# Where the weight buffers and working slots of a two-model forward pass lie in the on-chip memory

## The chip, the cores and the metric

The kernel runs on one core of one Trainium2 chip. The metric is the device time of one execution in microseconds (us). A core has a matrix engine (PE, TensorE), a vector engine (DVE), a scalar engine (ACT), a general engine (POOL) and a queue engine that issues transfers (SP). All of them read operands from the on-chip memory of 128 partitions; an address below is a byte offset within a partition, and the *phase* of a buffer is its address modulo 512.

## The reference

Two models of two layers each run one behind the other on 512 tokens of width 1024, everything in float32. What takes the time is matrix products of the activations with some 300 MB of weights.

```
for l in range(DEPTH):                                   # first model
    h = rmsnorm(x, g_mix); z = h @ w_in
    ya = sliding_window_sink_attention(aq, ak, av, sinks) @ w_a
    yb = (retention(rq, rk, rv) * silu(rg)) @ w_b
    x = x + (sigmoid(ga) * ya + sigmoid(gb) * yb) @ w_out
    x = x + square(relu(rmsnorm(x, g_mlp) @ w_up)) @ w_down
x = rmsnorm(x, g_final)
for l in range(DEPTH):                                   # second model
    y = hybrid_mixer(x, ...)     # top-k attention and gated linear attention
    x = layer_norm(ALPHA * x + y)
    y = conv_ffn(x, ...)         # width 2816, a causal convolution of 3 taps, gelu
    x = layer_norm(ALPHA * x + y)
```

## The kernel before

**Products in three parts.** A float32 product is made of three matmuls of type float32r. Each operand is split into a rounded high part and a low remainder: for activations `xh`, `xl` (`split`, L456 to L466), for weights `hi`, `lo`. A step of a product adds w_hi·xh, w_hi·xl and w_lo·xh into one PSUM bank.

**Two forms of product.** In `fm` the weights are stationary: a step (`k_step`, L395 to L397) loads 128x128 weights and streams 512 tokens of `xh` or `xl` past them (in places only 256 tokens). One output tile of a product over 1024 inputs is 8 steps, that is 24 matmuls, and uses exactly one piece of weights. In `tm` the activations are stationary and 256 columns of weights stream (L448 to L450); one output tile there, too, is 24 matmuls, and uses two pieces, the first for steps 0 to 3 and the second for steps 4 to 7. In the profile's rows a matmul's form is written out<-moving,stationary: `pm<-xh,hi` is a step of `fm`, `pm<-hi,xh` one of `tm`.

**Where weights lie.** A piece of weights is 128x1024 floats. A transfer on SP's queue brings two pieces into one of two `raw` buffers. `split_next` then makes `hi` (ACT, L331) and `lo` (DVE or POOL, L332). The *plain* pieces go round four pairs of buffers of 4096 bytes: the i-th plain piece lies in pair i mod 4, counted from 0. When all four pairs are taken, a piece goes into four working slots instead (`whi`, `wlo`, L341 and L342). A working slot is 2048 bytes; there are 75, and everything else lives in them, above all each `xh` and `xl`.

**Addresses.** The eight weight buffers are pools of their own, with padding between them, so that they start at eight different phases from the start of the first: `WT_PHASE = (0, 32, 64, 128, 256, 384, 448, 480)`, the first four for `hi` of pairs 0 to 3, the last four for `lo`. The built program puts the first at 40352, which is phase 416, and the slots at 73632, also phase 416. Since slots are 2048 bytes long, every slot has phase 416. Relative to any slot, pair 0 lies at 0 (`hi`) and 256 (`lo`), pair 1 at 32 and 384, pair 2 at 64 and 448, pair 3 at 128 and 480. A step within a piece moves the stationary operand by 512 bytes, so its phase stays that of its buffer.

**Order.** The order on every engine is the order in which the program is written (`manual_schedule`). Each stage writes the matmuls of its products with the work of the other parts (attention, retention, norms) pumped between output tiles; nothing in that order depends on addresses. Buffers are handed out in rotation as they come free.

Of the kernel before, what the change touches and what calls it, by code (L numbers as in the profile page):

```python
# [12 lines left out]
F = mybir.dt.float32  # L13
FR = mybir.dt.float32r
# [5 lines left out]
P = 128  # L20
# [6 lines left out]
HI_BUFS = 4  # L27
RAW_BUFS = 2
AHEAD_1, AHEAD_2 = 9, 11
WT_PHASE = (0, 32, 64, 128, 256, 384, 448, 480)  # L30
TOP_ROUNDS = 2
NSLOT = 75
FT = 22
GROUPS = ((0, 6), (6, 14), (14, 22))
ALPHA = (2.0 * DEPTH) ** 0.25
# [111 lines left out]
class Small:  # L147


    def __init__(self):  # L150
        self.parts, self.at, self.n = [], {}, 0
# [103 lines left out]
class Net:  # L255
    def __init__(self, nc, tc, pools, meta, w):
        self.nc, self.tc, self.meta, self.w = nc, tc, meta, w
        self.pools = pools
        self.uid = 0
        self.pump = Pump()  # L260
        self.lo_pool = False
        cols = meta["pieces"]
        self.piece_cols = cols
        self.chunk_off, off = [], 0
        self.chunk_cols = []
        for i in range(0, len(cols), 2):
            n = sum(cols[i : i + 2])
            self.chunk_off.append(off)
            self.chunk_cols.append(n)
            off += n * P  # L270
        self.n_dma = self.n_split = self.n_use = 0
        self.raw, self.ready = {}, {}
        self.n_plain = 0
        self.plain = set()
        self.ahead = HI_BUFS
        self.post, self.due, self.later = deque(), [], []
# [35 lines left out]
    def split_next(self, done, pool=False):  # L312


        i = self.n_split
        if i >= len(self.piece_cols):
            return
        c, j = i // 2, i % 2
        while self.n_dma <= min(c + RAW_BUFS - 1, len(self.chunk_off) - 1):
            self.dma_next()  # L320
        o = self.piece_cols[i - 1] if j else 0
        n = self.piece_cols[i]
        raw = self.raw[c][:, o : o + n]
        e = self.nc.gpsimd if pool or self.lo_pool else self.nc.vector
        self.plain = {q for q in self.plain if q >= done}
        if len(self.plain) < HI_BUFS:
            j = self.n_plain % HI_BUFS
            self.n_plain += 1
            hi = self.pools["wt"][j].tile([P, 1024], FR, tag="hi", name=self.name("hi"))
            lo = self.pools["wt"][HI_BUFS + j].tile([P, 1024], FR, tag="lo", name=self.name("lo"))  # L330
            self.nc.scalar.copy(hi[:, :n], raw)  # L331
            e.tensor_tensor(lo[:, :n], raw, hi[:, :n].bitcast(F), op=ALU.subtract)  # L332
            his = [hi[:, :512], hi[:, 512:]]
            los = [lo[:, :512], lo[:, 512:]]
            self.plain.add(i)
        else:
            his, los = [self.s(FR, "whi") for _ in range(2)], [self.s(FR, "wlo") for _ in range(2)]
            for q in range(2):
                r = raw[:, 512 * q : min(512 * q + 512, n)]
                m = r.shape[1]  # L340
                self.nc.scalar.copy(his[q][:, :m], r)  # L341
                e.tensor_tensor(los[q][:, :m], r, his[q][:, :m].bitcast(F), op=ALU.subtract)  # L342
        self.ready[i] = (his, los)
        self.n_split += 1
# [1242 lines left out]
def emit(nc, meta, arrays, stop=None):  # L1587
    ins = {}
    for n, a in arrays.items():
        ins[n] = nc.dram_tensor(n, a.shape, mybir.dt.from_np(a.dtype), kind="ExternalInput").ap()  # L1590
    out = nc.dram_tensor("out", (P, NK, T), F, kind="ExternalOutput").ap()
    with tile.TileContext(nc) as tc:
        with (
            tc.tile_pool(name="raw", bufs=RAW_BUFS) as raw,
            tc.tile_pool(name="const", bufs=1) as const,
            tc.tile_pool(name="tiny", bufs=40) as tiny,
            tc.tile_pool(name="main", bufs=2, space=PSUM) as main,
            tc.tile_pool(name="side", bufs=6, space=PSUM) as side,
            ExitStack() as stack,
        ):  # L1600
            smalls = const.tile([P, arrays["small"].shape[1]], F, name="smalls")
            wt = []
            at = 0

            def pad(n):
                if n:
                    stack.enter_context(tc.tile_pool(name=f"pad{len(wt)}_{n}", bufs=1)).tile([P, n // 4], F, name=f"pad{len(wt)}_{n}")

            for i, ph in enumerate(WT_PHASE):
                pad((ph - at) % 512)  # L1610
                at = ph
                wt.append(stack.enter_context(tc.tile_pool(name=f"wt{i}", bufs=1)))
            pad(-at % 512)
            with tc.tile_pool(name="s", bufs=NSLOT) as sp, tc.manual_schedule():
                pools = dict(raw=raw, wt=wt, const=const, tiny=tiny, main=main, side=side, s=sp)
                net = Net(nc, tc, pools, meta, ins["w"])
                x = [net.s(base="x") for _ in range(NK)]
                net.smalls = smalls
                g0 = const.tile([P, NK], F, name="g0")
                o, n = meta["small"]["g_mix0"]  # L1620
                nc.sync.dma_start(g0, ins["small"][:, o : o + n])
                nc.sync.dma_start(x[0], ins["x"][:, 0, :])
                net.dma_next(True)
                for k in range(1, 4):
                    nc.sync.dma_start(x[k], ins["x"][:, k, :])
                net.dma_next()
                for k in range(4, NK):
                    nc.sync.dma_start(x[k], ins["x"][:, k, :])
                nc.sync.dma_start(smalls, ins["small"])
                net.pos = ins["pos"]  # L1630
                net.ident, net.ones = net.small("ident"), net.small("ones")
                net.tables_1(ins["big"], ins["band"])
                net.ones_r, net.suffix = [const.tile([P, P], FR, name=n) for n in ("ones_r", "suffix_r")]
                net.halves = const.tile([P, 32], FR, name="halves_r")
                nx = {"xs": [None] * 8}
                nx["xs"][0] = net.split(x[0], g0[:, 0:1])
                for _ in range(2):
                    net.split_next(0)
                for k in range(1, NK):
                    nx["xs"][k] = net.split(x[k], g0[:, k : k + 1])  # L1640
                    if k < 7:
                        nx["acc"] = net.sumsq(x[k - 1], nx.get("acc"))
                net.split_next(0)
                for k in range(6, NK):
                    nx["acc"] = net.sumsq(x[k], nx["acc"], nc.vector)
                net.split_next(0)
                nc.scalar.copy(net.ones_r, net.ones)
                nc.scalar.copy(net.suffix, net.small("suffix"))
                nc.scalar.copy(net.halves, net.small("halves"))
                for l in range(DEPTH):  # L1650
                    nx = net.layer_1(l, x, nx)
                xs, iq = nx
                for l in range(DEPTH):
                    xs, iq = net.layer_2(l, xs, iq, ins["wg"], out if l + 1 == DEPTH else None)
# [10 lines left out]
```

## Time and profile before

| | |
|---|---|
| time, median of 3 runs | 3425.09 us (3424.93 to 3425.33) |
| profiled execution | 3424.1 us |
| its span, first to last instruction | 3422.3 us |
| PE busy | 3377.3 us (99%) |
| DVE, ACT, POOL busy | 1969.8, 1293.5, 656.6 us |
| mean granted PE clock | 0.996 |
| transferred | 295.93 MB, 86 GB/s on average |

Matmuls overlap: a row's duration of one matmul includes what it shares with its neighbours, and its end is modelled. The time that a matmul costs is the distance from its start to the start of the next. A stretch that runs from the first matmul of an output tile to the first matmul of the next is therefore the time of one tile, and the rows below are cut that way.

### The profile page before, as it was taken

The numbers are of one execution on the slowest core, as the hardware profiler recorded it, in microseconds if no ns is written. First come the engines' busy times: TensorE is split into PE (matmuls) and PEld (weight loads), VectorE is DVE, ScalarE is ACT, GpSimd is POOL, SyncE is SP. The second block draws the span as 40 slices with busy tenths as digits, with TensorE's granted clock in tenths as the row PEclk, the third lists the DMA queues.
The fourth block names the chain that finished last, engine by engine and source line by source line (L and its number), as shares of the span: only waits on it lengthen the run. The fifth ranks groups of instructions, "written<-read, shape, count | busy, mean of one in ns | idle before, by whom it ended". The sixth has DMA issues, their size and how long they took to land.

```text
span 3422.3 us, 43082 instructions
## 1 busy us (share of the span) xinstructions
PE 3377.3 (99%) x17450; PEld 2813.5 (82%) x17450; DVE 1969.8 (58%) x3435; ACT 1293.5 (38%) x2206; POOL 656.6 (19%) x447
## 2 busy tenths in 40 slices
PE   9999999999999999999999999999999999999997
PEld 7888888887888888889988778888889777888887
DVE  7555543456555553356885447555778844575466
ACT  3433333233333333233533343343354333443342
POOL 5100000123100010030551014210146400232113
PEclk9999999999999999999999999999999999999999
DMA  4222222232122222231222131223212112312230
GB/s 149 75 74 86 87 99 99 93 127 76 50 74 74 99 101 88 98 125 62 75 74 74 62 123 50 87 99 123 99 52 75 64 73 74 124 46 90 99 135 25
DMA packets 44935, 295.93 MB, mean 86 GB/s; under 512 B 5120, under 2 KB 7296, under 8 KB 10816
## 3 DMA queue, kind: packets, MB, share of 16 engines
q1 hardware_dynamic: 44496, 292.66, 23.6%
q8 instruction: 137, 2.24, 0.3%
q14 instruction: 62, 0.51, 0.0%
q10 hardware_dynamic: 160, 0.26, 0.0%
q0 software_dynamic: 80, 0.26, 0.0%
HBM read 291.06 MB, written 2.10 MB: 86 GB/s over the span
## 4 chain that ended last, share of the span: by engine, by line
PE 93%; DVE 5%; issue 1%; ACT 1%; POOL 0%; DMA 0%; DVEq 0%; SPq 0%; ACTq 0%; POOLq 0%
PE pm L395 23%; PE pm L397 22%; PE pm L396 22%; PE ps L397 3%; PE ps L395 3%; PE ps L396 3%; PE pm L448 3%; PE pm L450 2%; PE pm L449 2%; PE ps L544 2%; PE ps L403 1%; PE ps L1091 1%; DVE s L1011 1%; PE ps L404 1%; PE ps L405 1%
## 5 line engine op out<-in xcount | busy, mean ns | idle before, releaser
L395 PE MATMUL pm<-xh,hi 128*128 128x512 f32 (+1 forms) x3056 | 1201.5, 393 | 3.7 <-DVE c L1410 3.1
L397 PE MATMUL pm<-xh,lo 128*128 128x512 f32 (+1 forms) x3056 | 1193.6, 391 | 0.4 <-DVE lo L332 0.4
L396 PE MATMUL pm<-xl,hi 128*128 128x512 f32 (+1 forms) x3056 | 1189.6, 389 | 1.6 <-DVE xl L1563 1.2
L395 PEld LDWEIGHTS pm<-xh,hi 128*128 128x128 f32 x3056 | 574.7, 188 | 134.7 <-issue 12.0
L396 PEld LDWEIGHTS pm<-xl,hi 128*128 128x128 f32 x3056 | 573.9, 188 | 128.3 <-DVE xl L1563 3.2
L397 PEld LDWEIGHTS pm<-xh,lo 128*128 128x128 f32 x3056 | 573.5, 188 | 128.2 <-DVE lo L332 0.8
L332 DVE TENSOR_TENSOR lo<-raw,hi 128x1024 fp32r<-128x1024 f32 (+1 forms) x413 | 515.7, 1251 | 174.8 <-ACT hi L331 173.7
L331 ACT CAST hi<-raw 128x1024 fp32r<-128x1024 f32 (+1 forms) x469 | 483.3, 1036 | 211.0 <-PE pm L396 168.8
L448 PE MATMUL pm<-hi,xh 128*128 128x256 f32 x768 | 219.3, 286 | 1.0 <-DVE s L1009 0.6
L450 PE MATMUL pm<-hi,xl 128*128 128x256 f32 x768 | 216.1, 281 | 0.0
L449 PE MATMUL pm<-lo,xh 128*128 128x256 f32 x768 | 215.1, 280 | 0.0
L395 PE MATMUL pm<-xh,whi 128*128 128x512 f32 (+1 forms) x512 | 186.8, 365 | 4.0 <-DVE s L537 4.0
L396 PE MATMUL pm<-xl,whi 128*128 128x512 f32 (+1 forms) x512 | 186.2, 364 | 0.8 <-DVE xl L1563 0.5
L397 PE MATMUL pm<-xh,wlo 128*128 128x512 f32 (+1 forms) x512 | 185.5, 362 | 0.0
L1418 POOL TENSOR_TENSOR c<-c,c 128x512 f32<-128x512 f32 x44 | 84.4, 1919 | 509.1 <-DVE c L1410 486.3
L332 POOL TENSOR_TENSOR lo<-raw,hi 128x1024 fp32r<-128x1024 f32 x56 | 140.0, 2504 | 128.1 <-ACT hi L331 87.1
L448 PEld LDWEIGHTS pm<-hi,xh 128*128 128x128 f32 x768 | 144.9, 189 | 8.2 <-issue 2.6
L395 PE MATMUL ps<-xh,hi 128*128 128x512 f32 (+1 forms) x384 | 139.0, 362 | 7.4 <-ACT hi L331 7.4
L449 PEld LDWEIGHTS pm<-lo,xh 128*128 128x128 f32 x768 | 145.4, 189 | 0.2
L450 PEld LDWEIGHTS pm<-hi,xl 128*128 128x128 f32 x768 | 144.6, 188 | 0.0
L501 POOL TENSOR_TENSOR s<-s,s 128x512 f32<-128x512 f32 x26 | 35.1, 1351 | 569.6 <-ACT s L498 569.3
L1409 DVE SCALAR_TENSOR_TENSOR c<-pm,smalls,c 128x511 f32<-128x511 f32 x82 | 61.4, 749 | 140.7 <-ACT c L1408 140.6
(318 smaller groups left out, 4784.6 us busy)
## 6 DMA issues: line engine op xcount, KB each, us to landing
raw<-w SPq DMA_DIRECT2D x265, 1024.0 KB, 4.8
raw<-w SPq DMA_DIRECT2D x7, 768.0 KB, 4.4
x<-x SPq DMA_DIRECT2D x8, 256.0 KB, 6.8
out<-acc SPq DMA_DIRECT2D x16, 128.0 KB, 1.8
raw<-w SPq DMA_DIRECT2D x2, 896.0 KB, 4.5
s<-big SPq DMA_DIRECT2D x6, 256.0 KB, 5.9
raw<-w SPq DMA_DIRECT2D x2, 512.0 KB, 5.3
smalls<-small SPq DMA_DIRECT2D x1, 462.5 KB, 7.7
```

The costliest lines, as they stand in the source:

```text
L331: self.nc.scalar.copy(hi[:, :n], raw)
L332: e.tensor_tensor(lo[:, :n], raw, hi[:, :n].bitcast(F), op=ALU.subtract)
L395: mm(ps[:, ts], lhsT=w1, rhs=xh[:, ts], start=first, stop=False)
L396: mm(ps[:, ts], lhsT=w1, rhs=xl[:, ts], start=False, stop=False)
L397: mm(ps[:, ts], lhsT=w2, rhs=xh[:, ts], start=False, stop=last)
L448: self.nc.tensor.matmul(ps[:, :256], lhsT=x1, rhs=w1, start=(k == 0), stop=False)
L449: self.nc.tensor.matmul(ps[:, :256], lhsT=x1, rhs=w2, start=False, stop=False)
L450: self.nc.tensor.matmul(ps[:, :256], lhsT=x2, rhs=w1, start=False, stop=(k == NK - 1))
L501: (e or self.nc.gpsimd).tensor_tensor(acc, acc, sq, op=ALU.add)
L544: self.nc.tensor.transpose(dst[:, i * P : (i + 1) * P], src, self.ident)
L1409: nc.vector.scalar_tensor_tensor(c[:, 1:], ps[:, : T - 1], w[1], c[:, 1:], op0=ALU.mult, op1=ALU.add)
L1418: nc.gpsimd.tensor_tensor(a, a, c, op=ALU.mult)
```

## The change

The eight pools and the padding between them go. One padding of 96 bytes takes their place, then one pool of four `hi` buffers and one of four `lo` buffers. The built program now puts the `hi` buffers at 40448 and on, the `lo` buffers at 56832 and on, and the slots at 73216 and on, all at phase 0. Relative to any slot every weight buffer lies at 0. The raw buffers, the constants and the small tables stay where they were (`raw` and `smalls` at phase 128). What was saved on padding makes room for a 76th slot.

Every engine has the same instructions in the same order with the same shapes, and the i-th plain piece still goes to the buffer i mod 4. Since 76 slots go round in place of 75, a new tile takes another slot than before, and some writes on DVE, ACT and POOL wait for another engine's release; no wait of a PE or SP instruction changes.

```diff
-WT_PHASE = (0, 32, 64, 128, 256, 384, 448, 480)
+PAD = 24
 TOP_ROUNDS = 2
-NSLOT = 75
+NSLOT = 76
...
         if len(self.plain) < HI_BUFS:
-            j = self.n_plain % HI_BUFS
-            self.n_plain += 1
-            hi = self.pools["wt"][j].tile([P, 1024], FR, tag="hi", name=self.name("hi"))
-            lo = self.pools["wt"][HI_BUFS + j].tile([P, 1024], FR, tag="lo", name=self.name("lo"))
+            hi = self.pools["hi"].tile([P, 1024], FR, tag="hi", name=self.name("hi"))
+            lo = self.pools["lo"].tile([P, 1024], FR, tag="lo", name=self.name("lo"))
...
-            for i, ph in enumerate(WT_PHASE):
-                pad((ph - at) % 512)
-                at = ph
-                wt.append(stack.enter_context(tc.tile_pool(name=f"wt{i}", bufs=1)))
-            pad(-at % 512)
+            stack.enter_context(tc.tile_pool(name="pad", bufs=1)).tile([P, PAD], F, name="pad")
+            hi = stack.enter_context(tc.tile_pool(name="hi", bufs=HI_BUFS))
+            lo = stack.enter_context(tc.tile_pool(name="lo", bufs=HI_BUFS))
```

## Rows read from the trace of the kernel before

**Rows 1.** The page: busy time by engine, and the chain that ended last.

```profile
PE 3377.3 (99%) x17450; PEld 2813.5 (82%) x17450; DVE 1969.8 (58%) x3435; ACT 1293.5 (38%) x2206; POOL 656.6 (19%) x447
...
PE 93%; DVE 5%; issue 1%; ACT 1%; POOL 0%; DMA 0%; DVEq 0%; SPq 0%; ACTq 0%; POOLq 0%
```

**Rows 2.** Stretches: from:to, length, busy us (instructions) by engine, clock, DMA share, GB/s.

```profile
817.00:830.00 13.00, 9.04 (x37) 7.08 (x36) 13.00 (x16) 4.71 (x7) 11.41 (x9) 0.95 0.22 82
830.00:1744.00 914.00, 913.82 (x4834) 771.19 (x4834) 504.31 (x920) 327.26 (x577) 143.32 (x100) 1.00 0.24 85
1744.00:1784.00 40.00, 35.90 (x212) 29.27 (x213) 37.26 (x58) 15.83 (x28) 25.14 (x13) 0.96 0.21 76
...
2654.00:2706.00 52.00, 47.51 (x306) 39.54 (x305) 47.91 (x90) 19.75 (x36) 27.51 (x14) 0.97 0.23 82
```

**Rows 3.** Waits of PE, first two: line and what for, us, times, longest us.

```profile
PE ps L1198 <- DVE S L1188: 7.6, 2, 3.8
PE ps L395 <- ACT hi L331: 7.4, 1, 7.4
```

**Rows 4.** PE in four tiles of `fm`: pieces 47 to 50, pairs 3, 0, 1, 2.

```profile
334.22:339.78 5.57, 5.57 (x25) 1.00 0.14 18
339.78:345.23 5.45, 5.45 (x25) 1.00 0.42 174
345.23:350.80 5.57, 5.57 (x25) 1.00 0.09 25
350.80:356.36 5.56, 5.56 (x25) 1.00 0.40 168
```

**Rows 5.** PE in a tile of `fm` with its weights in slots.

```profile
729.17:734.62 5.45, 5.45 (x25) 1.00 0.45 177
```

**Rows 6.** Timeline of the same stretch, its first matmul: start us, us.

```profile
729.17 0.39 PE L395 MATMUL pm<-xh,whi 128*128 128x512 f32 x1
```

**Rows 7.** Groups by line and form: instructions, busy us, mean ns of one.

```profile
L395 PE MATMUL pm<-xh,hi 128*128 128x512 f32 x2968 | 1176.2, 396 | 3.7 <-DVE c L1410 3.1 <-DVE s L537 0.6
...
L448 PE MATMUL pm<-hi,xh 128*128 128x256 f32 x768 | 219.3, 286 | 1.0 <-DVE s L1009 0.6 <-ACT V L1305 0.4
...
L395 PE MATMUL pm<-xh,whi 128*128 128x512 f32 x376 | 147.9, 393 | 4.0 <-DVE s L537 4.0
...
L395 PE MATMUL ps<-xh,hi 128*128 128x512 f32 x264 | 105.3, 399 | 7.4 <-ACT hi L331 7.4
...
L395 PE MATMUL ps<-xh,whi 128*128 128x512 f32 x88 | 34.3, 389 | 0.0
...
L395 PE MATMUL ps<-xh,hi 128*128 128x256 f32 x120 | 33.7, 281 | 0.0
...
L395 PE MATMUL pm<-xh,hi 128*128 128x256 f32 x88 | 25.4, 288 | 0.0
```

**Rows 8.** Timeline, a tile of `tm` on pairs 0 and 1: start us, us.

```profile
131.60 0.28 PE L448 MATMUL pm<-hi,xh 128*128 128x256 f32 x1
...
133.04 0.28 PE L448 MATMUL pm<-hi,xh 128*128 128x256 f32 x1
...
134.47 0.38 PE L544 MATMUL ps<-smalls,s 128*128 128x128 f32 x2
```

**Rows 9.** Timeline, a tile of `tm` on pairs 2 and 3.

```profile
108.66 0.28 PE L448 MATMUL pm<-hi,xh 128*128 128x256 f32 x1
...
111.47 0.38 PE L544 MATMUL ps<-smalls,s 128*128 128x128 f32 x2
```

**Rows 10.** Timeline of DVE: `lo` of pieces 48 and 51, pairs 0 and 3.

```profile
333.02 1.23 DVE L332 TENSOR_TENSOR lo<-raw,hi 128x1024 fp32r<-128x1024 f32 x1 [0.25 <-ACT hi L331]
...
347.76 1.23 DVE L332 TENSOR_TENSOR lo<-raw,hi 128x1024 fp32r<-128x1024 f32 x1 [1.64 <-ACT hi L331]
```

**Rows 11.** Timeline of PE: float32 matmuls on slots, two to a row.

```profile
199.08 0.59 PE L661 MATMUL ps<-rv,s 128*128 128x256 f32 x2
199.51 0.59 PE L665 MATMUL ps<-rv,s 128*128 128x256 f32 x2
```

More of the change, by code (lines that the diff above doesn't have):

```diff
@@ L272, in __init__ @@
         self.raw, self.ready = {}, {}
-        self.n_plain = 0
         self.plain = set()
@@ L1601, in emit @@
             smalls = const.tile([P, arrays["small"].shape[1]], F, name="smalls")
[L1602 to L1607, printed above, removed]
-            for i, ph in enumerate(WT_PHASE):
-                pad((ph - at) % 512)
-                at = ph
-                wt.append(stack.enter_context(tc.tile_pool(name=f"wt{i}", bufs=1)))
-            pad(-at % 512)
+            stack.enter_context(tc.tile_pool(name="pad", bufs=1)).tile([P, PAD], F, name="pad")
+            hi = stack.enter_context(tc.tile_pool(name="hi", bufs=HI_BUFS))
+            lo = stack.enter_context(tc.tile_pool(name="lo", bufs=HI_BUFS))
             with tc.tile_pool(name="s", bufs=NSLOT) as sp, tc.manual_schedule():
-                pools = dict(raw=raw, wt=wt, const=const, tiny=tiny, main=main, side=side, s=sp)
+                pools = dict(raw=raw, hi=hi, lo=lo, const=const, tiny=tiny, main=main, side=side, s=sp)
                 net = Net(nc, tc, pools, meta, ins["w"])
```

## The prediction, made before the changed kernel ran

> **What bounds the kernel now.** I read the busy times and the chain first: PE is busy in 99% of the span, and the chain that ended last is PE for 93% [rows 1]. The cut by stretches says where this doesn't hold [rows 2]: in a long one (914 us) PE is idle for 0.2 us and DVE busy for 504, while at 817, 1744 and 2654 us DVE is busy for nearly all of the stretch and PE misses about 4 us in each. All of PE's idle time is 3422.3 - 3377.3 = 45 us [rows 1], and its two costliest waits come to 7.6 us and to 7.4, the latter once, at the start [rows 3]. The granted clock is 1.00 in the long stretch, that is 2.4 GHz, so nothing is to be had there. What is left is the distance from one matmul to the next. The change alters no matmul, so the question is whether that distance depends on where operands lie.
>
> It does, and the kernel before shows it, since its four pairs of buffers lie at four different phases relative to the slots. In four output tiles in a row, each 24 equal matmuls without an interruption, pair 0 takes 5.45 us and pairs 3, 1 and 2 take 5.57, 5.57 and 5.56 [rows 4]. DMA traffic doesn't explain it: it is heavy (168 to 174 GB/s) in the tile of pair 0 and in that of pair 2. Where the weights lie in slots (0 relative to the streamed slot, as all weights will after the change) a tile takes 5.45 as well [rows 5]; that it is a slot tile is seen in the form of its matmuls [rows 6]. So relative phases 0 and 256 cost 5.45 / 24 = 227 ns a matmul, the others 232 ns. In the long undisturbed stretches the 5 ns repeat with each round of four tiles.
>
> **Edit 1: the weight buffers go to relative phase 0; stationary weights, 512 tokens.** This form on plain buffers has 2968 + 264 = 3232 steps of three matmuls [rows 7], or 404 tiles of 8 steps; the other two lines of a step have the same counts. A quarter of them is on pair 0 and stays. 303 tiles are on pairs 1 to 3 and go from (5.57 + 5.57 + 5.56) / 3 = 5.567 to 5.45: 303 x 0.117 = 35.4 us less. With the rounding of the rows, 0.11 to 0.12 a tile, it is 33 to 36. Where other matmuls stand between the steps the saving per matmul is the same, since PE is the bound there as well. The 376 + 88 = 464 steps on slots [rows 7] stay.
>
> **Edit 2: the same for streamed weights.** Here the sign turns round. 768 steps [rows 7] make 96 tiles. One on pairs 0 and 1 takes 134.47 - 131.60 = 2.87 us, its half on pair 0 alone 133.04 - 131.60 = 1.44 [rows 8]; one on pairs 2 and 3 takes 111.47 - 108.66 = 2.81 [rows 9]. Relative phases 0 and 256 are thus the slowest here, and all tiles go to 2 x 1.44 = 2.88. The mean of the two kinds is 2.84, so the price is 96 x 0.04 = 3.8 us; between 1 us (all like the first kind) and 6.7 (all like the second). The steps of `fm` with 256 tokens are of the same length: 120 + 88 = 208 on plain buffers [rows 7], three quarters of them off pair 0, 468 matmuls at up to 0.07 / 24 = 2.9 ns, so 0 to 1.4 us; I take 0.7.
>
> **Edit 3: the absolute phase.** Slots and `xh`, `xl` go from phase 416 to 0. No matmul of the trace streams from phase 0. I take it as free, because pair 0's `lo` lies at 160 and its `hi` at 416, and tiles on both have one speed, that of the slots at 416. The bounds come from the nearest rows on both sides: every tile as slow as pairs 1 to 3, or every matmul as fast as the shortest distance at this length. The latter: in float32 pairs of matmuls start every 0.43 us [rows 11], 216 ns each, against 227. Both ends are rivals below.
>
> **Edit 4: DVE, ACT, POOL, the 76th slot and two pools.** Making `lo` takes DVE 1.23 us for pair 0 and for pair 3 [rows 10], although input `hi` and output `lo` lie at different phases in the two; I take the same for ACT and POOL. So these engines' instructions keep their length, and nothing is added to them. The bound is the same share as on PE, 2% either way, which idle time on all three hides. Changed waits on slots: zero, covered by DVE at 58% and ACT at 38% of the span [rows 1]; if the cover fell, it would be seen as a new wait of PE, whose costliest wait after the start is now 3.8 us long [rows 3]. Order and rotation are unchanged, so no wait goes and none takes its place.
>
> **What is lost of the gain.** In the three stretches where DVE sets the pace (13 + 40 + 52 = 105 us) a faster PE only waits longer; the gain, some 1% of PE's time, is lost there: 1 us. Shorter stretches at stage ends may lose half a microsecond. 1.5 in all. If slack elsewhere is smaller than it seems, up to 10; PE is idle for 45 us now [rows 1], so more would need a new kind of wait. In the stretches with a wait the clock was already below 1.00 (0.95 to 0.97) [rows 2]; a wait longer by 0.3 us adds no new one.
>
> **The sum.** -35.4 + 3.8 + 0.7 + 1.5 = -29.4 us. The profiled execution took 3424.1 us (span 3422.3 and 1.8 around it), giving 3394.7. The median of the runs, 3425.1, is 1.0 above it: 3395.7, rounded to **3396 us**. By the bounds of its own terms (-36 to -33; 1 to 6.7; 0 to 1.4; 1 to 10) the forecast runs from 3391 to 3410.
>
> **One rule against the row.** The four tiles show that the distance depends on the place of the weights [rows 4]. The Trainium skill, "TensorE: Matmul & The Clock Gate", Part 2, says of the step that loads weights: "Loading the next tile's weights doesn't steal SBUF read bandwidth from the running matmul", since the two operands have read ports of their own. By it the placing of weights would change nothing, and the time would stay at 3425. The trace disagrees by 0.12 us a tile.
>
> **The rivals.**
> *Absolute phases decide (slower).* The mechanism: each operand costs by its own address, and 160 and 416 (both 160 modulo 256) happen to be good ones, while 0 is like its neighbours 480 and 32, where `hi` of pairs 2 and 3 lies. Then pair 0 and the slots lose what they have: 101 tiles and 464 / 8 = 58, 159 x 0.12 = 19 us more, pairs 1 to 3 stay, giving 3444. For it: phase 0 is nowhere in the trace. Against it: in `fm` with pair 0 moving and stationary operands are at one phase modulo 256, in `tm` too, and the one form is fastest there and the other slowest, which a price per operand explains badly. The point from which it decides: the mean tile is now (159 x 5.45 + 303 x 5.567) / 462 = 5.527, and 6 us of other terms over 462 tiles are 0.013, so a tile after above 5.51 us makes it slower.
> *The gain goes nowhere.* Either 29 us come back as waits of PE, or the distance is set by neither phase. About 3425, within 3418 to 3432. For it: DVE-paced stretches exist [rows 2]. Against it: they are 105 us of 3422, and the tiles of 5.45 recur in the long stretches.
> *Phase 0 is better still.* If a part of the 227 ns comes from operands that start off some boundary, phase 0 takes it away, in `fm` and `tm`. At the 216 ns of [rows 11]: 462 tiles x 24 x 11 ns = 122 us and 96 x 24 x 11 ns = 25 us, 3396 - 147 = 3249; less for a part. Against it: those float32 matmuls stream from phase 416 as well and are not slowed.
>
> **How the numbers follow.** The forecast gets 0.73, the slower case 0.12, the faster one 0.08, no change 0.07. The range of 8 in 10 takes the forecast's own with a few microseconds below and the case of no change above it: 3385 to 3430. A measurement of this kernel tells 0.2% (7 us) from no change. Faster by more: 0.73 + 0.08 = 0.81; within: 0.07; slower: 0.12.
>
> **What would show it.** Undisturbed tiles of `fm` at 5.45 us for all four pairs, with no fourth that stands out; tiles of `tm` at 2.88; the three groups of `fm` on plain buffers with a mean ns that falls to that of the groups on slots; DVE, ACT and POOL as busy as before; PE's idle time within 3 us of the 45 now, its costliest wait that on L1198. Wrong, if any pair's tile is above 5.51 us (absolute phases), if tiles are below 5.40 (a boundary), or if tiles are 5.45 and PE's idle time grows by more than 10 us (the gain lost).

## The result, and the profile after

The changed kernel takes 3393.65 us (median of 4 runs, 3393.09 to 3394.25) against 3425.01 for the kernel before beside it: a ratio of 0.9909, interval 0.9897 to 0.9921, 31.4 us less. 3396 was forecast, within 3385 to 3430.

The page of the changed kernel: span, busy time by engine, and the chain that ended last.

```profile
span 3392.5 us, 43066 instructions
...
PE 3348.3 (99%) x17450; PEld 2818.3 (83%) x17450; DVE 1965.2 (58%) x3435; ACT 1292.1 (38%) x2206; POOL 657.0 (19%) x447
...
PE 92%; DVE 5%; issue 1%; ACT 1%; POOL 0%; DMA 0%; DVEq 0%; SPq 0%; ACTq 0%; POOLq 0%
```

Against [rows 1] PE is busy for 29.0 us less with the same 17450 matmuls, and the other engines differ by less than 5 us. The span fell by 29.8 us. PE's idle time is 3392.5 - 3348.3 = 44.2 us where it was 45.0: nothing has come back as a wait, and nothing was gained by waiting less.

The same four pieces as in [rows 4], after: from:to of one output tile, its length, PE busy (instructions), clock, DMA share, GB/s.

```profile
333.23:338.67 5.44, 5.44 (x25) 1.00 0.18 26
338.67:344.11 5.44, 5.44 (x25) 1.00 0.40 167
344.11:349.55 5.44, 5.44 (x25) 1.00 0.11 17
349.55:354.99 5.44, 5.44 (x25) 1.00 0.44 181
```

No tile stands out any more; all four pairs are where pair 0 was, and 0.01 us below it. Streamed weights, a tile that stood on pairs 2 and 3 and one that stood on pairs 0 and 1 (to be read against [rows 9] and [rows 8]; start us, us):

```profile
109.06 0.28 PE L445 MATMUL pm<-hi,xh 128*128 128x256 f32 x1
110.50 0.28 PE L445 MATMUL pm<-hi,xh 128*128 128x256 f32 x1
111.94 0.27 PE L541 MATMUL ps<-smalls,s 128*128 128x128 f32 x1
...
132.25 0.28 PE L445 MATMUL pm<-hi,xh 128*128 128x256 f32 x1
133.69 0.28 PE L445 MATMUL pm<-hi,xh 128*128 128x256 f32 x1
135.13 0.38 PE L541 MATMUL ps<-smalls,s 128*128 128x128 f32 x2
```

Both take 2.88 us, each half 1.44: slower than 2.81 and 2.87 before, as was forecast for this form. In the groups by line and form (instructions, busy us, mean ns) the plain buffers have come near the slots, and the streamed ones have gone up from 286 ns in [rows 7]:

```profile
L392 PE MATMUL pm<-xh,hi 128*128 128x512 f32 x2968 | 1167.9, 394 | 3.8 <-DVE c L1407 3.0 <-DVE s L534 0.7
...
L445 PE MATMUL pm<-hi,xh 128*128 128x256 f32 x768 | 221.0, 288 | 0.8 <-DVE s L1006 0.7
...
L392 PE MATMUL pm<-xh,whi 128*128 128x512 f32 x376 | 147.7, 393 | 4.1 <-DVE s L534 4.1
```

PE's waits are the old ones (line waited for, us in total, times, longest us), to be read against [rows 3]:

```profile
PE ps L1195 <- DVE S L1185: 7.6, 2, 3.8
PE ps L392 <- ACT hi L328: 7.3, 1, 7.3
```

Since both kernels run the same matmuls in the same order, the distance from each matmul's start to the next can be set one against the other. Summed over the two traces, in us (the second row holds the tiles that border on other work as well as those that have it between their steps):

| form, weights | matmuls | before | after | difference | per matmul |
|---|---|---|---|---|---|
| stationary, 512 tokens, pairs 1 to 3, tiles without interruption | 4104 | 951.7 | 930.3 | -21.3 | -5.2 ns |
| the same, all other tiles | 3144 | 749.4 | 736.7 | -12.7 | -4.0 ns |
| stationary, 512 tokens, pair 0 and slots | 3840 | 886.0 | 885.1 | -0.8 | -0.2 ns |
| stationary, 256 tokens | 1728 | 215.6 | 216.8 | +1.2 | +0.7 ns |
| streamed | 2304 | 287.3 | 291.2 | +4.0 | +1.7 ns |
| all other matmuls | 2330 | 314.2 | 314.0 | -0.1 | |

### The profile page after: what moved, and what is told of

Same layout as the page of the kernel before. It is cut to its first block, busy times and chain, and to the rows that moved or that the text cites. A ratio compares the mean times of both kernels' runs of the same rounds, so it can differ in the third digit from the quotient of the medians.

```text
span 3392.5 us, 43066 instructions
## 1 busy us (share of the span) xinstructions
PE 3348.3 (99%) x17450; PEld 2818.3 (83%) x17450; DVE 1965.2 (58%) x3435; ACT 1292.1 (38%) x2206; POOL 657.0 (19%) x447
## 4 chain that ended last, share of the span: by engine, by line
PE 92%; DVE 5%; issue 1%; ACT 1%; POOL 0%; DMA 0%; DVEq 0%; SPq 0%; ACTq 0%; POOLq 0%
PE pm L392 22%; PE pm L393 22%; PE pm L394 22%; PE ps L392 3%; PE ps L394 3%; PE ps L393 3%; PE pm L445 3%; PE pm L446 3%; PE pm L447 3%; PE ps L541 2%; PE ps L400 1%; PE ps L1088 1%; DVE s L1008 1%; PE ps L401 1%; PE ps L402 1%
## 5 line engine op out<-in xcount | busy, mean ns | idle before, releaser
L394 PE MATMUL pm<-xh,lo 128*128 128x512 f32 (+1 forms) x3056 | 1180.7, 386 | 0.4 <-DVE lo L329 0.4
```

The source lines that it names most:

```text
L394: mm(ps[:, ts], lhsT=w2, rhs=xh[:, ts], start=False, stop=last)
```

## The experiments

The theory was that the distance between matmuls depends on the phase of the weights relative to the other operand, modulo 256. Its rival was that each operand counts by its own address, so that multiples of 512 are good as such. Tiles below are output tiles without interruption, their length from first matmul to first matmul; where a distance in ns is given it is the median of the starts in the trace.

### Each half of the change alone

The change does two things: it puts weights and slots at one phase, and it makes that phase 0. The first alone takes the padding out of the changed kernel:

```diff
-PAD = 24
...
-NSLOT = 76
+NSLOT = 75
...
-            stack.enter_context(tc.tile_pool(name="pad", bufs=1)).tile([P, PAD], F, name="pad")
```

> One half of the change alone: the eight weight buffers in two pools without padding, 75 slots, so that weights and slots all lie at phase 416 in place of 0. If only the phase of the two operands relative to each other counts, all tiles take 5.45 us (weights stationary) and 2.88 us (weights streamed), and the time is that of the changed kernel, 3394 us within 2. If lying at multiples of 512 is what helps, or the 76th slot, this half brings at most a part: between 3400 and 3425.

It took 3394.38 us (3394.28 to 3395.15), a ratio of 0.9913 (0.9898 to 0.9928). The four tiles, everything at phase 416:

```profile
332.37:337.81 5.44, 5.44 (x25) 1.00 0.11 15
337.81:343.25 5.44, 5.44 (x25) 1.00 0.43 178
343.25:348.69 5.44, 5.44 (x25) 1.00 0.10 14
348.69:354.13 5.44, 5.44 (x25) 1.00 0.45 184
```

The second alone puts the padding of 96 bytes ahead of the eight pools of the kernel before:

```diff
+PAD = 24
...
             at = 0
+            stack.enter_context(tc.tile_pool(name="pad", bufs=1)).tile([P, PAD], F, name="pad")
```

> The other half alone: the eight buffers of the kernel before at their eight phases relative to the slots, the whole shifted by 96 bytes so that the slots lie at multiples of 512; 75 slots. If only the relative phase counts, nothing changes against the kernel before: 3425 us within 2, pair 0 at 5.45 us a tile and pairs 1 to 3 at 5.57. If the start of the slots counts, most of the gain is here: 3394 to 3410.

It took 3424.54 us (3423.16 to 3424.88), a ratio of 0.9999 (0.9989 to 1.0009). Pairs 3, 0, 1, 2:

```profile
334.33:339.89 5.56, 5.56 (x25) 1.00 0.21 29
339.89:345.34 5.45, 5.45 (x25) 1.00 0.39 162
345.34:350.91 5.57, 5.57 (x25) 1.00 0.15 26
350.91:356.47 5.56, 5.56 (x25) 1.00 0.40 166
```

The whole gain is in the first half. The multiples of 512 and the 76th slot together are worth at most the 0.7 us between this half and the changed kernel; both the slower and the faster rival, which hung on the absolute phase, fall here.

### Modulo 256

This kernel and the three others below that set `WT_PHASE` are the kernel before, with its eight pools, behind the padding of 96 bytes that puts the slots at phase 0.

```diff
-WT_PHASE = (0, 32, 64, 128, 256, 384, 448, 480)
+WT_PHASE = (256, 256, 256, 256, 256, 256, 256, 256)
+PAD = 24
...
```

> All weight buffers at relative phase 256, slots at phase 0. If the relative phase counts modulo 256, this is the changed kernel: tiles of 5.44 to 5.45 us with stationary weights and 2.88 with streamed ones, 3394 us. If modulo 512, tiles with stationary weights take some 5.56 and the time is near 3435.

One run took 3395.2 us, and its streamed matmuls are 120 ns apart as in the changed kernel. A tile with stationary weights, also as there:

```profile
263.31:268.75 5.44, 5.44 (x25) 1.00 0.10 29
```

### A map of phases

Two kernels put `hi` and `lo` of the four pairs at other multiples of 32; two more start from the changed kernel with 75 slots, use buffers that are 256 bytes longer and write a piece some bytes further into them, which allows any multiple of 4.

```diff
+WT_PHASE = (96, 160, 192, 0, 96, 160, 192, 0)      # the first
+WT_PHASE = (32, 64, 128, 224, 32, 64, 128, 224)    # the second
+PAD = 24
...
+PROBE = (4, 44, 52, 60)      # the third, in floats: 16, 176, 208, 240 bytes
+PROBE = (1, 46, 50, 62)      # the fourth: 4, 184, 200, 248 bytes
...
+            f = PROBE[self.n_plain % HI_BUFS]
+            hi, lo = hi[:, f : f + 1024], lo[:, f : f + 1024]
```

> A map of relative phases: pairs 0 to 3 lie, hi and lo alike, at 96, 160, 192 and 0 behind the slots, which lie at phase 0. If the relative phase counts modulo 256, a tile with stationary weights takes 5.45 us on pair 3 and some 5.56 to 5.60 on the others; with streamed weights pairs 2 and 3 share a tile, whose half on pair 3 takes 1.44 and the other half 1.38 to 1.42. If each operand counts by its own address, 160 modulo 256 is a good one, and pair 1 takes 5.45 as well. Time near 3425.

> The map's other half: pairs 0 to 3 at 32, 64, 128 and 224 behind the slots, hi and lo alike, so that no pair lies at 0. By the relative phase all four tiles with stationary weights take 5.54 to 5.60 us and those with streamed weights 2.75 to 2.85; against the changed kernel 404 tiles x 0.12 = 48 us more and 96 x 0.07 = 7 less: some 3435 us. If it lies near 3394 the relative phase is not the cause.

> A finer map: pairs 0 to 3 at 16, 176, 208 and 240 bytes behind a multiple of 256, hi and lo alike, slots at phase 0. If the distance changes smoothly with the phase, 16 and 240 take between 5.44 and 5.60 us a tile with stationary weights, and 176 and 208 lie near the 5.51 of 192. If any offset from 0 costs the whole, 16 and 240 take 5.56 or more. With streamed weights 192 was the fastest of the multiples of 32 (half a tile 1.36 us); 176 or 208 beats it or does not. Time between 3415 and 3445.

> The finest map: pairs 0 to 3 at 4, 184, 200 and 248 bytes behind a multiple of 256. Stationary weights at 240 took 5.48 us a tile, at 0 5.44, at 16 5.60. If the distance changes byte by byte, 248 lies between 5.44 and 5.48 and 4 between 5.44 and 5.60, nearer to 5.44; if it changes in steps of 16 bytes, 248 is 5.48 and 4 is 5.44. 184 and 200 lie near the 5.51 of 192. With streamed weights 192 at 113 ns a matmul stays the fastest, or 184 or 200 goes below.

Single runs of 3430.07, 3441.87, 3421.26 and 3439.55 us. The second is 7 us above the 3435 expected: its 512-token matmuls on plain buffers cost 53.6 us more than in the changed kernel where 48 were set, and the streamed ones 5.0 less where 7 were. The first kernel's tiles at 0, 96, 160 and 192, and under them the fourth's at 248, 4, 184 and 200:

```profile
334.29:339.74 5.45, 5.45 (x25) 1.00 0.09 15
339.74:345.36 5.62, 5.62 (x25) 1.00 0.43 172
345.36:350.98 5.61, 5.61 (x25) 1.00 0.13 23
350.98:356.48 5.51, 5.51 (x25) 1.00 0.41 171
```

```profile
336.45:342.05 5.60, 5.60 (x25) 1.00 0.14 29
342.05:347.62 5.57, 5.57 (x25) 1.00 0.38 159
347.62:353.19 5.57, 5.57 (x25) 1.00 0.19 29
353.19:358.73 5.54, 5.54 (x25) 1.00 0.40 164
```

All measured phases behind a multiple of 256 (median length of a tile with stationary weights, two figures where the lengths fall apart, and the median distance of streamed matmuls, lowest and highest of the three lines):

| phase, bytes | 0 | 4 | 16 | 32 | 64 | 96 | 128 | 160 |
|---|---|---|---|---|---|---|---|---|
| stationary, us a tile | 5.44 | 5.57 | 5.44 or 5.60 | 5.60 | 5.60 | 5.62 | 5.57 | 5.61 |
| streamed, ns a matmul | 119 to 120 | 123 | 118 to 119 | 117 | 118 | 118 to 119 | 118 to 119 | 117 to 118 |

| phase, bytes | 176 | 184 | 192 | 200 | 208 | 224 | 240 | 248 |
|---|---|---|---|---|---|---|---|---|
| stationary, us a tile | 5.52 | 5.57 | 5.51 | 5.54 | 5.56 | 5.60 | 5.44 to 5.49 | 5.60 |
| streamed, ns a matmul | 117 to 120 | 120 | 114 to 116 | 120 | 119 | 117 to 118 | 116 to 117 | 118 to 122 |

Phase 0 is the best for stationary weights, and 4 bytes off it cost 0.13 us a tile. At 16 the phase alone doesn't fix the length: of 63 tiles without interruption 22 take 5.44 us and 41 take 5.59 or 5.60. Two such tiles of the third kernel, on the same weight buffers, the same slots and the same PSUM bank:

```profile
361.50:367.10 5.60, 5.60 (x25) 1.00 0.44 183
383.66:389.10 5.44, 5.44 (x25) 1.00 0.53 193
```

At 240 a quarter of the tiles take 5.44 and most 5.48 or 5.49, again on the same addresses. The pace goes with that of the tile before: of the tiles at 16 that follow one at 240, the 18 short ones all follow one of 5.44 to 5.46 us, the 30 long ones all follow one of 5.48 or more. So something beside the operands' addresses counts at these two phases and carries over from tile to tile; what it is stays open. The expectation of a smooth change fails: 248 is slower than 240 and 192 both, and 4 is nowhere near 0. Nor did it go in steps of 16 bytes. With streamed weights 4, 184 and 200, which are no multiples of 16, are not below 120 in any line, and 248 in one alone. 192 is the fastest there; the kernel before had it only for `lo` of pair 2 (448).

### Which load it is

```diff
-WT_PHASE = (0, 32, 64, 128, 256, 384, 448, 480)
+WT_PHASE = (0, 0, 0, 0, 128, 128, 128, 128)
+PAD = 24
...
```

> The hi buffers at relative phase 0, the lo buffers at 128, slots at phase 0. With stationary weights a step runs hi, hi, lo. If the streaming matmul collides with the load that is under way for the next matmul, the second of the three is slow (its next load is lo): 227, 232, 227 ns from start to start. If a matmul's distance depends on its own weights, the third is slow: 227, 227, 232. Either way one of three is slow: 404 tiles x 8 x 5 ns = 16 us more than the changed kernel, 3410 us.

One run took 3428.5 us, and neither expectation held. The three matmuls of a step (hi, hi, lo) are 227, 232 and 234 ns from their successors: the second, whose next load is off phase, and the third, whose own weights are. A tile of this kernel:

```profile
341.06:346.61 5.55, 5.55 (x25) 1.00 0.38 160
```

5.55 us is 0.11 above the changed kernel, 404 x 0.11 = 44 us if every tile ran without interruption, where 16 was expected. 34.8 were measured: the 512-token matmuls on plain buffers cost 39.2 us more, and the streamed ones, 118 to 119 ns apart in place of 120, 4.1 less. So one buffer off phase spoils two of the three matmuls. The records of the loads (instructions, busy us, mean ns), first the load of `hi` that runs under the third matmul, then that of `lo`:

```profile
L396 PEld LDWEIGHTS pm<-xh,hi 128*128 128x128 f32 x3056 | 584.9, 191 | 139.9 <-issue 12.1 <-ACT hi L332 0.3
...
L398 PEld LDWEIGHTS pm<-xh,lo 128*128 128x128 f32 x3056 | 573.8, 188 | 118.0 <-DVE lo L333 0.8
```

In the changed kernel all three loads of a step take 188 ns. The load of the buffer off phase has no longer record, then, and the one behind it is 3 ns longer. Whether the load is delayed in the one matmul and the stream in the next, or both in both, that doesn't tell, and it stays open.

### A version that beats both

Streamed weights and stationary ones want different phases. Buffers of 4352 bytes alternate between phases 0 and 256, and pieces of one kind are written 192 bytes further:

```diff
+OFF = 48
+PIECES = ((14, 22), (144, 152), (256, 264), (269, 281), (289, 293), (333, 341), (401, 409), (414, 426), (434, 438), (478, 486), (546, 550))
...
-            hi = self.pools["hi"].tile([P, 1024], FR, tag="hi", name=self.name("hi"))
+            hi = self.pools["hi"].tile([P, 1088], FR, tag="hi", name=self.name("hi"))
...
+            f = OFF if any(a <= i < b for a, b in PIECES) else 0
+            hi, lo = hi[:, f : f + 1024], lo[:, f : f + 1024]
```

> The changed kernel, but pieces that are streamed, or used with 256 tokens, are written 192 bytes further into buffers that are 256 bytes longer; all others stay at relative phase 0 (modulo 256). 75 slots. If the best phase depends on the form alone, 96 tiles with streamed weights go from 2.88 to 2.72 us (15 us) and 208 steps of 256 tokens lose 3 x 6 ns each (4 us): 3375 us. If the phase counts through what lies in the neighbouring buffers, or modulo 512, the gain is absent: 3394 or more.

It took 3382.05 us (3380.46 to 3382.72), a ratio to the kernel before of 0.9875 (0.9858 to 0.9891), 7 us more than the 3375 expected. A tile of streamed weights, its halves and its end:

```profile
107.78 0.28 PE L449 MATMUL pm<-hi,xh 128*128 128x256 f32 x1
109.14 0.28 PE L449 MATMUL pm<-hi,xh 128*128 128x256 f32 x1
110.50 0.27 PE L545 MATMUL ps<-smalls,s 128*128 128x128 f32 x1
```

2.72 us in place of 2.88, as expected; all streamed matmuls together fell from 291.2 to 278.4 us, 12.8 of the 15 expected. The 256-token form brought 0.4 us (216.8 to 216.4) of the 4 expected. Its 624 matmuls on plain pieces fell from 79.7 to 77.6 us, and its 1104 on slots rose from 137.2 to 138.8. Most of that rise is the clock: behind a stretch in which PE missed 0.9 us, the granted clock fell to 0.50, that is 1.2 GHz, and 14 of these matmuls stand 213 ns apart in place of 120, 1.3 us in all. Two stretches in this kernel, and the matching ones in the changed kernel, where the clock stayed:

```profile
2445.00:2450.30 5.30, 4.44 (x37) 1.00 0.00 2
2450.40:2453.40 3.00, 3.00 (x16) 0.50 0.00 0
...
2454.00:2459.20 5.20, 4.69 (x39) 1.00 0.00 2
2459.30:2462.30 3.00, 3.00 (x28) 1.00 0.00 0
```

Without it the form would have brought 0.4 + 1.3 = 1.7 us, by estimate. The last run leaves its pieces at 0:

```diff
-PIECES = ((14, 22), (144, 152), (256, 264), (269, 281), (289, 293), (333, 341), (401, 409), (414, 426), (434, 438), (478, 486), (546, 550))
+PIECES = ((14, 22), (144, 152), (269, 281), (289, 293), (414, 426), (434, 438))
```

> As the kernel with 192 bytes for two kinds of pieces, but only pieces that are streamed lie 192 bytes further; those used with 256 tokens go back to 0. Measured there: 12.8 us less for streamed weights and 0.4 for 256 tokens, where 4 were expected. If the 256-token pieces bring nothing, this takes 3382 us, within 2, as that one; if they do bring 4 us and another loss hides it, 3386.

It took 3383.01 us (3381.94 to 3383.38) against 3382.05: the ranges of both overlap. Nearly all of the gain is in the streamed pieces. Between two matmuls of 256-token pieces the median distance did fall from 120 to 114 ns; whether that is worth 1 or 2 us of the whole, these runs can't tell.

## Why the prediction was right

**The place was right, and shown before.** That one tile in four was shorter, and that a tile on slots was as short, [rows 4] and [rows 5] said without an experiment. The two halves of the change run alone have shown that the relative phase is the cause and not the address, which was only argued before.

**Edit 1** was set at -35.4 us and measured at -21.3 - 12.7 - 0.8 = -34.8. Its step on interrupted tiles was wrong in detail: "the saving per matmul is the same" there; it is 4.0 ns against 5.2. In 73 of these tiles the 24 matmuls run on end, with other work before and behind them. Their second to fourth distance (median) is 231, 232 and 232 ns before and 233, 231 and 233 after, so the change saves nothing there. That the sum is right to 0.6 us is partly luck, since undisturbed tiles end at 5.44, not at the 5.45 that was taken. The 0.01 us is one matmul: in the kernel before, the last of a tile on pair 0, which runs while weights of pair 1 are loaded, is 235 ns from its successor (median), and 227 after the change. So the tiles on pair 0 gained too, where the prediction let them stay.

**Edit 2** was set at 3.8 and measured at 4.0; the 256-token form, set at 0.7 within 0 to 1.4, at 1.2. The sign, opposite to that of edit 1, came from reading the second form separately. The mean was taken over two kinds of tile, on pairs 0 and 1 and on pairs 2 and 3; 32 of the 96 tiles lay on pairs 1 and 2 or 3 and 0, at 2.84 and 2.82 us. That these are near the mean of the other two was luck.

**Edit 3** was taken at nothing, and was nothing: a kernel with everything at phase 416 is 0.7 us from one with everything at 0.

**Edit 4** held: DVE, ACT and POOL are busy as before, PE has the same waits, and the kernel with 75 slots is 0.7 us away. Its step "I take the same for ACT and POOL" holds for the phases of this change, but not for POOL at any address. In the kernel with `hi` and `lo` at 4, 184, 200 and 248, no multiples of 16, POOL's subtraction is shorter than in the kernel before (mean ns), while its other instructions keep their length:

```profile
L332 POOL TENSOR_TENSOR lo<-raw,hi 128x1024 fp32r<-128x1024 f32 x56 | 140.0, 2504 | 128.1 <-ACT hi L331 87.1 <-DVE t L1053 10.1 <-DVE S L1188 9.4
...
L334 POOL TENSOR_TENSOR lo<-raw,hi 128x1024 fp32r<-128x1024 f32 x56 | 117.6, 2101 | 144.0 <-ACT hi L333 110.5 <-DVE S L1190 9.4 <-issue 8.0
```

**What is lost** was set at 1.5 us and is the term that failed, by little: PE's idle time didn't grow, it fell by 0.8 us. The sum of the matmuls' distances gives -29.7 us, and the span fell by 29.8. The median fell by 31.4, 1.6 more than the span of the two profiled executions.

**The rule against the row.** The Trainium skill, "TensorE: Matmul & The Clock Gate", Part 2, says that loading the next weights takes no read bandwidth from the running matmul. As the prediction read it, that the placing of weights then changes nothing, it doesn't hold for these float32r operands: with the weights 4 bytes off the streamed operand's phase a tile takes 5.57 us against 5.44. The starts show distances and not bandwidth, so what load and stream share stays open. That the load overlaps the matmul agrees with the trace: in the changed kernel loads are busy for 2818.3 us and matmuls for 3348.3 of a span of 3392.5.

**Rivals.** The absolute phase, slower: the tile is at 5.44, below its point of decision of 5.51, and both halves speak against it. The gain lost in waits: idle time fell. The boundary, faster: tiles are not below 5.40. Its 216 ns, from float32 matmuls of 256 columns [rows 11], was no bound for float32r ones of 512.

## What to carry to other kernels

Before costing a change of addresses, look for instructions of one form that already run at several addresses: if their start-to-start distances differ, the price of those placements is in the trace. On PE, align the operand that is loaded and the operand that is streamed to each other, here to a multiple of 256 bytes for 512 columns; measure each form separately, since for 256 streamed columns that very phase was one of the slow ones. Look at single tiles beside their median: at phase 16 it hid two lengths. And before a missing gain is put down to the placing, compare the granted clock of the stretch. A few ns a matmul are lost to sight in the groups' means (396 against 394 ns) and plain in the lengths of whole tiles.

## What the runs showed of the hardware

The distance between float32r matmuls depends on the phase of weights and streamed operand relative to each other, and is the same at 0 and 256: 5.44 us for 24 matmuls there, up to 5.62 in between, with no smooth course (192: 5.51, 248: 5.60, 4: 5.57). At 16, tiles on the same addresses took 5.44 or 5.60 us, by the pace of the tile before, so the phase is not all that counts. For 256 columns the distance runs from 113 ns (all streamed pieces at 192) to 123 (at 4). The absolute phase of the slots didn't count at 0 and 416. A buffer 128 bytes off phase makes two matmuls long, the one under which it is loaded (232 ns against 227) and its own (234).

ACT's cast of a piece and DVE's subtraction on the same buffers kept their length, a median of 1.04 us and of 1.22 to 1.23 us on each of the four pairs, in the kernels before and after and in the four of the map. POOL's subtraction took a mean of 2.50 us before and 2.52 in the changed kernel, all buffers at multiples of 16 bytes, and 2.10 in the one kernel where none lay at one; the reason stays open.
